# Two input queues, pairwise sums of squares, earlier forget gates, a chunked mixer start and a PSUM sum in the tail, in one layer of a hybrid encoder

## The chip, the cores and the metric

The kernel runs on one core of one Trainium2 chip. The metric is the device time of one execution in microseconds, as the median of several runs. A core has five engines that each work through their own list of instructions in order: TensorE (PE, matmuls), VectorE (DVE), ScalarE (ACT), GpSimd (POOL) and SyncE (SP, here only for issuing DMAs). They wait for one another by semaphores.

## The reference

One layer for 512 prompt tokens and 64 sample tokens (T = 576), model width 1024. The sample tokens also attend to 1024 cached rows.

```
h = rmsnorm(x, g_attn)
q, k, v, f_lin, q_c, c_kv, k_r = split(h @ w_in)
logf = log_sigmoid(f_lin + b_f)                 # forget gates, 8 heads
F = cumsum(past logf, then logf)
fox = softmax(mask(q k^T / 8 + F[t] - F[s])) v  # 8 heads of 64
mla = latent attention with rotary key, from q_c, c_kv, k_r
x = x + concat(fox, mla) @ w_out
u = rmsnorm(x, g_ffn) @ w_up                    # gate | value, 2 x 2816
x = x + (silu(conv3(gate)) * conv3(value)) @ w_down
y = rmsnorm(x, final_norm)
outputs: y, and the new k, v, logf, latent, rope key, conv rows
```

## The kernel before

Everything is kept transposed: features lie on the 128 partitions, the 576 tokens along the free axis. The width 1024 is eight chunks of 128. Every fp32 product is made of three PE passes over split values: each operand is written as a high half (rounded, type fp32r) and a low half (the remainder), and `gemm` (L201) adds low x high, high x high and high x low in one PSUM bank. `hilo` (L192) splits a weight tile: ACT writes the high half (L194), DVE or POOL the low half (L135, chosen by the tables `ENG` and by counting). `split_scaled` does the same for activations, with the norm's gain multiplied in (L266 on ACT, L267 on DVE). Weight tiles arrive in two buffers `wr` and are split into two buffers `wh`.

The start: SP issues the loads of the eight input tiles `x_in`, of `par` (gains), of `w_krf` (rope key and forget weights) and of the first key weights `wk`, in turn, then constants `con`, cached keys and values, and further weights. As the chunks arrive they are split into `xs` tiles, and two gemms run chunk by chunk: the one with 72 columns for the rope key and the forget logits, and `k0`, the keys of the first pair of heads. ACT squares the eight chunks (L220), DVE and POOL add them up in two groups of four (L135), and `col_sums` (L230) adds over the partitions with a matmul against ones. `rstd` makes from this the factor R = 1/rms with Ln, Exp and one Newton step (L250 to L262); all evacuations of the projections multiply by R. While that runs, PE works on the next projections, which need no R.

`fox_gemm(p)` (L447) makes keys, queries and values of pair p of the eight FoX heads; `gates` (L559) turns the forget logits into log-sigmoid, its running sum by a scan, and the tile `cf`, whose high and low halves are added to the scores by matmuls (L523) with the selector `sl`. The scan of the cached forget values (L585) reads `sp`, loaded over the same buffer as `con`. `s_gemm` (L743), `s_scores`, `s_values` and others are generators that issue their work in small steps; a planner with costs mixes them, so that projection matmuls fill the gaps between score and value steps. The framework's scheduler then fixes the order on each engine. In this phase the projections write two PSUM banks named `g` in turn: a new gemm waits until DVE has evacuated the bank.

The mixer: after `w_out`, the eight chunks of x are split again (`x2hl`), the same norm is made (R2), and `up_conv` runs 44 tiles of `w_up`, gate and value alternately (tile ch and ch + 22). `down_group` collects the down projection. In the tail the last part of the down projection runs in two halves of the tokens (320 and 256), and for each of the eight output tiles m: DVE adds the PSUM result into x (L971), ACT squares it (L976), DVE adds to a running sum (L978), two matmuls against ones close the sum (L980, L981), then Ln, Exp and Newton make `r3`, and DVE (L996) or POOL (L993, L994) multiply and the result goes out by DMA (L997). In the second half POOL takes the tiles in `TPOOL`, here 0 and 1.

Of the kernel before, what the change touches and what calls it, by code (L numbers as in the profile page):

```python
# [7 lines left out]
F32 = mybir.dt.float32  # L8
# [7 lines left out]
P = 128  # L16
# [39 lines left out]
    "sq0": "a", "acc0": "gggvvv", "sq": "agv", "acc": "gvvv",  # L56
# [9 lines left out]
TPOOL = (0, 1)  # L66

W0 = 6
# [3 lines left out]
def build(nc, tc, io):  # L72
# [74 lines left out]
    S.preload_act_table_set("natural_log_exp_and_others")  # L147
    par = sb([P, N_PAR], F32, "par", 1)
    wkrf = sb([P, 1024], F32, "wr", 2)
    x_in = []  # L150
    for kc in range(8):
        xt = mixt()
        nc.sync.dma_start(xt[:, :T], io["xT"][:, kc, :])
        x_in.append(xt)
        if kc == 0:
            nc.sync.dma_start(par[:, :C_GF], io["par"][:, :C_GF])
            nc.sync.dma_start(wkrf[:, :144], io["w_krf"][:, :144])
            wk = sb([P, 1024], F32, "wr", 2)
        if kc == 1:
            nc.sync.dma_start(wkrf[:, 144:576], io["w_krf"][:, 144:])  # L160
            nc.sync.dma_start(wk[:, :512], io["w_in"][0][:, :512])
        if kc == 2:
            nc.sync.dma_start(wk[:, 512:], io["w_in"][0][:, 512:])
    nc.scalar.dma_start(par[:, C_GF:], io["par"][:, C_GF:])
# [36 lines left out]
    def gemm(ps, M, hl, acts, halves, by_chunk=False):  # L201
# [5 lines left out]
        for hf, kc in steps:  # L207
            o, w = halves[hf]
            for pi, (wi, xi) in enumerate(((0, 1), (0, 0), (1, 0))):
# [40 lines left out]
    def rstd_of(v, y, a, out):  # L250
        S.activation(y, v, AF.Ln)
        S.activation(y, y, AF.Exp, scale=-0.5)
        newton(v, y, a, out)

    def newton(v, y, a, out):
        V.tensor_tensor(a, y, y, op=ALU.mult)
        V.scalar_tensor_tensor(a, a, -0.5, v, op0=ALU.mult, op1=ALU.mult)
        V.scalar_tensor_tensor(out, a, 1.5, y, op0=ALU.add, op1=ALU.mult)

    def rstd(ps, n, out):  # L260
        v, y, a = (raw()[:, :T] for _ in range(3))
        evac(lambda d, p, c: V.tensor_scalar(d, p, 1.0 / n, EPS, op0=ALU.mult, op1=ALU.add), v, ps)  # L262
        rstd_of(v, y, a, out)
# [13 lines left out]
    for kc in range(8):  # L277
# [169 lines left out]
    def fox_gemm(p):  # L447
# [3 lines left out]
        G.dma_start(io["o_k"][p], k[:, :T])  # L451
        ps = in_tile(4 + p)
# [30 lines left out]
    def fox_setup(p, q, k, v):  # L483
# [14 lines left out]
        for hh in range(2):  # L498
            V.tensor_copy(sl[:, 64 * hh:64 * hh + 64], sel[:, 2 * p + hh:2 * p + hh + 1].to_broadcast([72, 64]))
# [598 lines left out]
```

## Time and profile before

| | |
|---|---|
| median of 3 runs | 811.48 us (809.47 to 812.81) |
| profiled execution | 810.69 us, span 808.9 us, mean granted clock 0.988 |
| PE busy | 772.8 us, 96% |
| DVE, ACT, POOL busy | 508.5, 340.6, 264.0 us |
| HBM read, written | 64.1 MB, 5.5 MB |

The page gives busy time per engine, the list of waits names for each engine whom it waited for, the timeline gives single instructions with the idle time ahead of them in brackets, and the table of stretches gives busy time and granted clock between two times. A clock of 1.00 is 2.4 GHz, 0.50 is 1.2 GHz. Times in the rows count from the start of the span.

### The profile page before, as it was taken

Reading aid. Unit: us, or ns where it says so; the run is one execution under the profiler, and the core shown is the slowest. Engines: PE = TensorE matmul, PEld = TensorE weight load, DVE = VectorE, ACT = ScalarE, POOL = GpSimd, SP = SyncE. Lnnn points to the kernel's source line nnn. Section 1 sums busy time; section 2 is a strip of 40 time slices with the busy share of each in tenths; the row PEclk is TensorE's granted clock in tenths of the full one; section 3 lists DMA queues with packets and bytes.
Section 4 is the critical chain, followed back from the end, with each engine's and each line's share of the span. In section 5 each row is a group of like instructions: output and inputs, shape, how many; then the busy total and the mean of one; then the engine's idle time right before and its main releaser. Section 6 shows DMA issues by size and latency. Waiting matters only on the chain.

```text
span 808.9 us, 14256 instructions
## 1 busy us (share of the span) xinstructions
PE 772.8 (96%) x5582; PEld 743.3 (92%) x5582; DVE 508.5 (63%) x941; ACT 340.6 (42%) x611; POOL 264.0 (33%) x390
## 2 busy tenths in 40 slices
PE   8898999999899989999999999999999999999994
PEld 8796899897789879999999999999999999999993
DVE  6838554878677763457867524676425667675356
ACT  7224652457667864124443212343113433433231
POOL 5134342336143230223333221433222343332034
PEclk9998999999999999999999999999999999999997
DMA  9373423545563741222222223222232222222313
GB/s 329 111 212 109 109 84 106 145 107 169 129 152 80 185 131 30 80 79 79 72 85 68 79 92 105 79 79 60 79 98 80 103 80 79 79 66 83 105 40 117
DMA packets 33811, 83.98 MB, mean 104 GB/s; under 512 B 6006, under 2 KB 9350, under 8 KB 33744
## 3 DMA queue, kind: packets, MB, share of 16 engines
q1 hardware_dynamic: 31520, 78.55, 32.6%
q0 software_dynamic: 1008, 3.19, 1.1%
q10 hardware_dynamic: 1216, 1.33, 0.5%
q8 instruction: 44, 0.72, 0.4%
q14 instruction: 23, 0.19, 0.1%
HBM read 64.12 MB, written 5.49 MB: 86 GB/s over the span
## 4 chain that ended last, share of the span: by engine, by line
PE 76%; DVE 10%; ACT 5%; DMA 3%; issue 3%; SPq 1%; POOL 1%; DVEq 0%; ACTq 0%; POOLq 0%
PE g L210 31%; PE s L210 19%; PE t L210 12%; PE g L438 3%; PE g L969 1%; DMA mix<-xT 1%; DVE B L382 1%; DVE xs L267 1%; PE s L720 1%; PE t L375 1%; ACT p L326 1%; PE s L969 1%; DMA A<-qr 1%; PE s L522 1%; DVE raw L135 1%
## 5 line engine op out<-in xcount | busy, mean ns | idle before, releaser
L210 PE MATMUL g<-xs,wh 128*128 128x288 f32 (+2 forms) x2028 | 281.1, 295 | 0.3 <-ACT spt L128 0.2
L210 PEld LDWEIGHTS g<-xs,wh 128*128 128x128 f32 x2028 | 271.1, 189 | 1.7 <-ACT spt L128 0.4
L194 ACT ACTIVATE wh<-wr 128x1024 fp32r<-128x1024 f32 (+4 forms) x106 | 99.8, 942 | 204.3 <-PE g L210 88.4
L135 POOL TENSOR_TENSOR wh<-wr,wh 128x1024 fp32r<-128x1024 f32 (+3 forms) x51 | 111.8, 2192 | 216.5 <-ACT wh L194 173.7
L210 PE MATMUL s<-xs,wh 128*128 128x320 f32 (+3 forms) x840 | 121.1, 300 | 2.3 <-DVE xs L267 2.3
L210 PEld LDWEIGHTS s<-xs,wh 128*128 128x128 f32 (+1 forms) x840 | 116.3, 188 | 2.7 <-ACT wh L194 1.8
L210 PE MATMUL t<-xs,wh 128*128 128x256 f32 (+3 forms) x576 | 83.9, 296 | 1.2 <-DVE xs L267 1.2
L210 PEld LDWEIGHTS t<-xs,wh 128*128 128x128 f32 (+1 forms) x576 | 79.1, 188 | 1.6 <-DVE xs L267 1.4
L135 DVE TENSOR_TENSOR wh<-wr,wh 128x1024 fp32r<-128x1024 f32 (+5 forms) x55 | 59.0, 1077 | 13.7 <-ACT wh L194 13.4
L892 POOL COPY KR<-raw 128x2 f32<-128x2 f32 x33 | 14.6, 443 | 94.1 <-DVE raw L890 94.1
L332 POOL TENSOR_SCALAR p<-p,small 128x128 f32<-128x128 f32 (+2 forms) x48 | 27.5, 575 | 50.9 <-DVE small L327 40.8
L896 DVE SCALAR_TENSOR_TENSOR raw<-raw,par 128x578 f32<-128x578 f32 x22 | 33.6, 1526 | 14.0 <-ACT raw L895 14.0
L326 ACT ACTIVATE p<-s,small 128x128 f32<-128x128 f32 (+1 forms) x64 | 33.6, 527 | 12.5 <-DVE small L361 9.2
L920 ACT ACTIVATE raw<-raw 128x578 f32<-128x578 f32 x22 | 15.1, 688 | 54.5 <-DVE raw L897 54.5
L382 DVE TENSOR_TENSOR B<-t,B 128x512 fp32r<-128x512 f32 (+1 forms) x64 | 29.9, 482 | 9.3 <-ACT B L128 9.2
L128 ACT ACTIVATE B<-t 128x512 fp32r<-128x512 f32 (+1 forms) x64 | 26.2, 435 | 17.1 <-PE t L375 16.4
L361 DVE TENSOR_REDUCE small<-s 128x1 f32<-128x128 f32 (+1 forms) x64 | 30.5, 480 | 4.3 <-PE s L359 2.9
L896 DVE SCALAR_TENSOR_TENSOR raw<-pq,par,raw 128x578 f32<-128x578 f32 x11 | 22.7, 2059 | 12.4 <-ACT raw L895 12.4
L375 PE MATMUL t<-ident,p 128*128 128x128 f32 x160 | 29.1, 277 | 1.0 <-DVE B L382 0.5
L890 DVE TENSOR_TENSOR raw<-s,R 128x256 f32<-128x256 f32 x22 | 9.3, 424 | 31.8 <-PE s L210 31.8
L438 PE MATMUL g<-spt,sv 128*128 128x128 f32 x216 | 26.7, 276 | 0.3 <-ACT spt L128 0.2
L438 PEld LDWEIGHTS g<-spt,sv 128*128 128x128 f32 x216 | 25.2, 192 | 1.1 <-ACT spt L128 0.6
(337 smaller groups left out, 1344.1 us busy)
## 6 DMA issues: line engine op xcount, KB each, us to landing
wr<-w_up SPq DMA_DIRECT2D x44, 512.0 KB
wr<-w_dn SPq DMA_DIRECT2D x24, 384.0 KB
wr<-w_in SPq DMA_DIRECT2D x16, 512.0 KB
A<-pq SPq DMA_DIRECT2D x32, 256.0 KB
mix<-xT SPq DMA_DIRECT2D x16, 288.0 KB
wr<-w_out SPq DMA_DIRECT2D x8, 512.0 KB
A<-pq SPq DMA_DIRECT2D x24, 128.0 KB
sk<-k_c SPq DMA_DIRECT2D x4, 512.0 KB
```

What stands on the lines that cost most here:

```text
L128: S.activation(dst, src, AF.Copy)
L135: (V if pick(kind) == "v" else G).tensor_tensor(dst, a, b, op=op)
L194: S.activation(hl[:, 0, a:b], r[:, a:b], AF.Copy)
L210: PE.matmul(ps[hf][:M, :w], lhsT=hl[:, wi, kc * M:(kc + 1) * M], rhs=acts[kc][:, xi, o:o + w], start=(kc == 0 and pi == 0), stop=(kc == n ...
L326: S.activation(p, src, AF.Exp, bias=nm, accum_out=sm[:, 0:1])
L332: (G if e == "g" else V).tensor_scalar(p, p, sm[:, 1:2], 1.0, op0=ALU.mult, op1=ALU.mult)
L361: V.reduce_max(nm[:, 0:1], s[:, :W], axis=AX.X, negate=True)
L375: PE.transpose(t[:, P * (i - j):P * (i - j + 1)], st["p"][i][:, P * j:P * (j + 1)], ident)
L382: V.tensor_tensor(ptj[:, 1, off:], t[:, :w], f(ptj[:, 0, off:]), op=ALU.subtract)
L438: PE.matmul(out, lhsT=v[:, j, :], rhs=spt[:, j, :], start=(j == 0), stop=(j == 8))
L896: V.scalar_tensor_tensor(t, u[:, 1:579], par[:, C_CW + 44 + ch:C_CW + 44 + ch + 1], t, op0=ALU.mult, op1=ALU.add)
L969: PE.matmul(ps[:, :w], lhsT=whl[m][:, wi, kc * P:(kc + 1) * P], rhs=g2[kc][:, xi, c], start=(kc == 0 and pi == 0), stop=(kc == n - 1 and p ...
```

## The change

1. The input comes by two queues: SP issues the eight input tiles, ACT issues `par`, `w_krf` and `wk`, ahead of its table load. The further weights on SP stand behind constants and caches.
2. The high halves of `wk` are written by POOL (`hilo` with `eng=G`). When chunks are taken one by one, the passes begin with high x high.
3. Squares are added by twos, all on DVE, and `col_sums` takes four tiles. `ident`, `bfc`, `sel` and the casts `sl` are made after R (`normed`).
4. `gates` runs between the keys and the queries of the second pair, in `mix` buffers.
5. `up_gemm` runs the mixer's tiles 0 and 22 chunk by chunk, with the norm's sums issued after the fourth chunk; the split x lies in buffers `sk`, `sv` and four of `xs`.
6. In the tail's second half the running sum lies in a PSUM bank, `r3` is written to PSUM and copied by ACT for POOL, and POOL takes three tiles.

```diff
-    "sq0": "a", "acc0": "gggvvv", "sq": "agv", "acc": "gvvv",
+    "sq0": "a", "acc0": "v", "sq": "agv", "acc": "gvvv",
-TPOOL = (0, 1)
+TPOOL = (0, 1, 2)
-W0 = 6
+W0 = 5
...
+    wk = sb([P, 1024], F32, "wr", 2)
+    nc.scalar.dma_start(par[:, :C_GF], io["par"][:, :C_GF])
+    nc.scalar.dma_start(wkrf[:, :144], io["w_krf"][:, :144])
+    nc.scalar.dma_start(wk[:, :512], io["w_in"][0][:, :512])
+    nc.scalar.dma_start(wkrf[:, 144:576], io["w_krf"][:, 144:])
+    nc.scalar.dma_start(wk[:, 512:], io["w_in"][0][:, 512:])
+    S.preload_act_table_set("natural_log_exp_and_others")
...
+        if eng is G:
+            G.tensor_scalar(hl[:, 0, a:b], r[:, a:b], 1.0, 1.0, op0=ALU.mult, op1=ALU.mult)
+        else:
+            S.activation(hl[:, 0, a:b], r[:, a:b], AF.Copy)
...
-            for pi, (wi, xi) in enumerate(((0, 1), (0, 0), (1, 0))):
+            for pi, (wi, xi) in enumerate(((0, 0), (0, 1), (1, 0)) if by_chunk else ((0, 1), (0, 0), (1, 0))):
...
-            hilo(hk, wk, 0, 512)
+            hilo(hk, wk, 0, 512, G)
-            hilo(hk, wk, 512, 1024)
+            hilo(hk, wk, 512, 1024, G)
...
-        rstd(col_sums([sq_sum([t[:, :T] for t in x_in[n:n + 4]], "sq0", "acc0") for n in (0, 4)]), D, R)
+        normed = rstd(col_sums([sq_sum([t[:, :T] for t in x_in[n:n + 2]], "sq0", "acc0") for n in (0, 2, 4, 6)]), D, R)
+    with tc.issue_after(normed):
+        V.tensor_copy(ident, con[:, K_ID:K_ID + P])
+        V.tensor_copy(bfc, con[:, 0:320])
+        V.tensor_copy(sel, con[0:72, K_SEL:K_SEL + 8])
...
         G.dma_start(io["o_k"][p], k[:, :T])
+        if between:
+            between()
         ps = in_tile(4 + p)
...
-            fx[p] = fox_gemm(p)
-            if p == 1:
-                gates()
+            fx[p] = fox_gemm(p, gates if p == 1 else None)
...
+    XT = [("sk", 2), ("sk", 2), ("sv", 2), ("sv", 2)] + [("xs", 8)] * 4
...
+    def up_gemm(chs):
+        hls = [wload(io["w_up"][ch], 1024) for ch in chs]
+        pss = [psg() for _ in chs]
+        for kc in range(8):
+            if kc == 4:
+                rstd(sumsq(x2), D, R2)
+            for hl, ps in zip(hls, pss):
+                for hf, (o, w) in enumerate(HB):
+                    for pi, (wi, xi) in enumerate(((0, 1), (0, 0), (1, 0))):
+                        PE.matmul(ps[hf][:, :w], lhsT=hl[:, wi, kc * P:(kc + 1) * P], rhs=x2hl[kc][:, xi, o:o + w],
+                                  start=(kc == 0 and pi == 0), stop=(kc == 7 and pi == 2))
+        return dict(zip(chs, pss))
...
+    early.update(up_gemm((0, NCH)))
...
+        run = bank("s")[:, :w] if hf else acc
...
-                    V.tensor_tensor(acc, acc, sq, op=ALU.add)
+                    V.tensor_tensor(acc if m == 6 else run, run, sq, op=ALU.add)
...
+        if hf:
+            newton(v, y, a, pn[:, :w])
+            S.activation(r3, pn[:, :w], AF.Copy)
+            r3, r3g = pn[:, :w], r3
```

How the built program stands, at three places. On POOL at the start, where the tiles are memory that is set to zero for later use, and `ISA` is an instruction that selects POOL's code library; before:

```order
L380 MEMSET B 128x2x128
L492 MEMSET sv 64x128
L135 ISA
L135 TENSOR_TENSOR raw<-raw 128x576
L583 DMA sp<-logf_c 8x1024
L135 TENSOR_TENSOR raw<-raw 128x576 x2
```

and after the change:

```order
L382 MEMSET B 128x2x128
L190 ISA
L190 TENSOR_SCALAR wh<-wr 128x512
L496 MEMSET sv 64x128
L190 TENSOR_SCALAR wh<-wr 128x512
L135 TENSOR_TENSOR wh<-wr,wh 128x1024
L588 DMA sp<-logf_c 8x1024
```

The library instruction now stands ahead of the high halves of `wk`, and the DMA of the cached forget values behind a weight split.

On DVE a few evacuations behind R, the last of which frees the bank `g` for the second pair's keys (`raw<-g,R` are evacuations of the projections, `pq` the split keys and queries); before:

```order
L450 TENSOR_TENSOR raw<-g,R 128x288
L454 SCALAR_TENSOR_TENSOR raw<-t,R 128x288
L454 SCALAR_TENSOR_TENSOR raw<-s,R 128x288
L135 TENSOR_TENSOR wh<-wr,wh 128x1024
L489 COPY sk<-raw 128x64
L467 TENSOR_TENSOR pq<-raw,pq 128x512
L457 TENSOR_TENSOR raw<-g,R 128x288
```

and after the change:

```order
L452 TENSOR_TENSOR raw<-g,R 128x288
L458 SCALAR_TENSOR_TENSOR raw<-t,R 128x288
L504 CAST sl<-sel 72x64 x4
L458 SCALAR_TENSOR_TENSOR raw<-s,R 128x288
L590 SCALAR_TENSOR_TENSOR spt<-sp,B 8x1024
L493 COPY sk<-raw 128x64
L567 SCALAR_TENSOR_TENSOR mix<-mix 8x576
L471 TENSOR_TENSOR pq<-raw,pq 128x512
L461 TENSOR_TENSOR raw<-g,R 128x288
```

The casts `sl`, the scan of the cached forget values (L590) and the first gate step (L567) now stand ahead of the evacuation that frees the bank `g`; the three copies of constants, not shown, stand directly behind R. Before, the copies, the casts and the scan stood ahead of R.

On PE between the cached-key scores of the first head (`s<-sk,qb`) and the matmul that adds the forget terms (`s<-cf,sl`); before:

```order
L522 MATMUL s<-sk,qb 128x320
L210 MATMUL g<-xs,wh 128x288 x144
L341 MATMUL t<-ident,raw 128x128 x4
L494 MATMUL t<-ident,raw 64x128
L210 MATMUL g<-xs,wh 128x288 x27
L341 MATMUL t<-ident,raw 128x128 x4
L210 MATMUL g<-xs,wh 128x288 x10
L494 MATMUL t<-ident,raw 64x128
L210 MATMUL g<-xs,wh 128x288 x11
L523 MATMUL s<-cf,sl 128x384 x2
```

and after the change:

```order
L527 MATMUL s<-sk,qb 128x320
L208 MATMUL g<-xs,wh 128x288 x72
L343 MATMUL t<-ident,raw 128x128 x4
L498 MATMUL t<-ident,raw 64x128
L528 MATMUL s<-cf,sl 128x384 x2
L528 MATMUL s<-cf,sl 128x320
L530 LDWEIGHTS bfc
L530 MATMUL s<-bfc 128x64
L208 MATMUL g<-xs,wh 128x288 x72
L520 MATMUL s<-A 128x256
```

The forget terms now follow 72 projection matmuls instead of 192, and 72 more stand behind them, ahead of the first head's own scores.

## Rows read from the trace of the kernel before

**Rows 1.** The page, busy us by engine: share of the span, instructions.

```profile
PE 772.8 (96%) x5582; PEld 743.3 (92%) x5582; DVE 508.5 (63%) x941; ACT 340.6 (42%) x611; POOL 264.0 (33%) x390
```

**Rows 2.** Waits of PE: for whom, us in total, times, longest.

```profile
PE s L523 <- DVE cf L590: 3.1, 1, 3.1
PE s L230 <- DVE raw L135: 2.9, 1, 2.9
...
PE t L210 <- DVE xs L267: 1.2, 1, 1.2
```

**Rows 3.** Stretches: us, busy by engine, granted clock, DMA share, GB/s.

```profile
24.50:27.70 3.20, 3.20 (x7) 2.32 (x8) 1.48 (x2) 0.00 (x0) 0.00 (x0) 0.50 0.31 92
73.00:79.00 6.00, 5.97 (x23) 4.54 (x23) 4.45 (x17) 3.08 (x10) 2.92 (x6) 0.50 0.47 132
180.00:320.00 140.00, 129.17 (x866) 113.61 (x865) 99.18 (x255) 96.80 (x247) 44.77 (x68) 1.00 0.48 128
```

**Rows 4.** Timeline of PE at the start: start us, us, instruction [idle before].

```profile
6.62 0.46 PE L210 MATMUL s<-xs,wh 128*72 128x288 f32 x2 [1.68 <-DVE xs L267]
...
24.44 3.24 PE L230 MATMUL s<-raw,ones 128*128 128x288 f32 x6 [2.89 <-DVE raw L135]
...
34.04 6.26 PE L210 MATMUL g<-xs,wh 128*128 128x288 f32 x46
```

**Rows 5.** Timeline of POOL at the start.

```profile
7.10 0.20 POOL L492 MEMSET sv<- 64x128 f32 x1
15.34 1.42 POOL L135 TENSOR_TENSOR raw<-raw 128x576 f32<-128x576 f32 x1 [8.03 <-ACT raw L220]
```

**Rows 6.** Timeline of DVE around R.

```profile
18.71 5.67 DVE L135 TENSOR_TENSOR raw<-raw 128x576 f32<-128x576 f32 x3
...
28.09 2.27 DVE L585 TENSOR_TENSOR_SCAN spt<-sp,B 8x1024 f32<-8x1024 f32 x1
...
32.63 0.45 DVE L320 TENSOR_TENSOR mix<-s,R 32x288 f32<-32x288 f32 x1
...
37.61 0.45 DVE L457 TENSOR_TENSOR raw<-g,R 128x288 f32<-128x288 f32 x1
...
40.34 0.46 DVE L457 TENSOR_TENSOR raw<-g,R 128x288 f32<-128x288 f32 x1 [1.67 <-PE g L210]
```

**Rows 7.** Line L499 alone: ns of one, least, median, most.

```profile
L499 DVE CAST sl<-sel x8: 179/186/1854, 15.4 to 96.3; 72x64 fp32r<-72x64 f32 x8
```

**Rows 8.** DMA in the first 30 us: a queue, and an issue with its landing.

```profile
q8 instruction: 1, 0.02, 0.2%
...
sp<-logf_c POOLq DMA_DIRECT2D x1, 32.0 KB, 5.9
```

**Rows 9.** Timelines of PE and DVE between R and the gates.

```profile
41.72 18.55 PE L210 MATMUL g<-xs,wh 128*128 128x288 f32 x137
...
59.34 0.74 DVE L562 SCALAR_TENSOR_TENSOR raw<-mix 8x576 f32<-8x576 f32 x1
```

**Rows 10.** Timelines of ACT and DVE, a weight split after the mixer's start.

```profile
384.38 1.06 ACT L194 ACTIVATE wh<-wr 128x1024 fp32r<-128x1024 f32 x1 [1.58 <-PE s L210]
...
385.47 1.23 DVE L135 TENSOR_TENSOR wh<-wr,wh 128x1024 fp32r<-128x1024 f32 x1 [0.29 <-ACT wh L194]
```

**Rows 11.** Timelines of DVE, PE, POOL and ACT in the tail.

```profile
796.05 1.02 DVE L978 TENSOR_TENSOR raw<-raw 128x256 f32<-128x256 f32 x1 [0.48 <-ACT raw L976]
796.99 0.41 DVE L971 TENSOR_TENSOR mix<-s,mix 128x256 f32<-128x256 f32 x1
797.12 0.70 PE L980 MATMUL o<-raw,ones 128*128 128x256 f32 x2 [1.54 <-DVE raw L978]
...
801.04 1.35 DVE L996 SCALAR_TENSOR_TENSOR v<-mix,par,v 128x256 f32<-128x256 f32 x2
801.17 1.79 POOL L994 TENSOR_TENSOR raw<-mix,v 128x256 f32<-128x256 f32 x2 [2.55 <-DVE v L258]
804.47 0.38 ACTq L997 DMA_DIRECT2D o_y<-raw  x1
```

More of the change, by code (lines that the diff above doesn't have):

```diff
@@ L154, in build @@
         x_in.append(xt)
[L155 to L164, printed above, removed]
+    nc.sync.dma_start(par[:, C_GF:], io["par"][:, C_GF:])
     con = sb([P, 1152], F32, "sp", 1)
@@ L252, in rstd_of @@
         S.activation(y, y, AF.Exp, scale=-0.5)
-        newton(v, y, a, out)
+        return newton(v, y, a, out)
     def newton(v, y, a, out):
@@ L257, in newton @@
         V.scalar_tensor_tensor(a, a, -0.5, v, op0=ALU.mult, op1=ALU.mult)
-        V.scalar_tensor_tensor(out, a, 1.5, y, op0=ALU.add, op1=ALU.mult)
+        return V.scalar_tensor_tensor(out, a, 1.5, y, op0=ALU.add, op1=ALU.mult).ins
     def rstd(ps, n, out):
@@ L262, in rstd @@
         evac(lambda d, p, c: V.tensor_scalar(d, p, 1.0 / n, EPS, op0=ALU.mult, op1=ALU.add), v, ps)
-        rstd_of(v, y, a, out)
+        return rstd_of(v, y, a, out)
     def split_scaled(dst, src, g):
@@ L445, in build, with fox_gemm @@
     mixes = [None] * 8
-    def fox_gemm(p):
+    def fox_gemm(p, between=None):
         ps = k0 if p == 0 else in_tile(p)
@@ L497, in fox_setup @@
         sl = sb([72, P], F32R, "sl", 2)
-        for hh in range(2):
-            V.tensor_copy(sl[:, 64 * hh:64 * hh + 64], sel[:, 2 * p + hh:2 * p + hh + 1].to_broadcast([72, 64]))
+        with tc.issue_after(normed):
+            for hh in range(2):
+                V.tensor_copy(sl[:, 64 * hh:64 * hh + 64], sel[:, 2 * p + hh:2 * p + hh + 1].to_broadcast([72, 64]))
         samples[p] = dict(sk=sk, sv=sv, qb=qb, sl=sl, mix=mix, cost=5, tags=SMP["F"])
@@ L560, in gates @@
         S.activation(z, z, AF.Identity, bias=bf)
-        mn = raw()[:8, :T]
+        mn = mixt()[:8]
         V.scalar_tensor_tensor(mn, z, -1.0, z, op0=ALU.mult, op1=ALU.min)
-        e = raw()[:8, :T]
+        e = mixt()[:8]
         S.activation(e, mn, AF.Exp)
-        up = raw()[:8, :T]
+        up = mixt()[:8]
         V.tensor_scalar(up, e, 1.0, None, op0=ALU.add)
@@ L877, in build @@
     R2 = sb([P, T], F32, "R", 1)
-    rstd(sumsq(x2), D, R2)
     cs = sb([P, 512], F32, "KR", 1)[:, :176].rearrange("p (a b) -> p a b", b=4)
-    def up_conv(ch):
-        hl = wload(io["w_up"][ch], 1024)
-        ps = psg()
-        gemm(ps, P, hl, x2hl, HB)
+    def up_gemm(chs):
[10 more added lines that the diff above has]
+        return dict(zip(chs, pss))
+    early = {}
+    def up_conv(ch):
+        ps = early.pop(ch, None)
+        if ps is None:
+            hl = wload(io["w_up"][ch], 1024)
+            ps = psg()
+            gemm(ps, P, hl, x2hl, HB)
         u = raw()
@@ L898, in up_conv @@
         return t
-    gslots = [("A", 2, 1), ("A", 2, 1), ("B", 2, 2), ("B", 2, 2)] + [(t, 2, 1) for t in ("sk", "sk", "sv", "sv")] + [(t, 1, 1) for t in ("cf", "sp", "spt")]
+    gslots = [("A", 2, 1), ("A", 2, 1), ("B", 2, 2), ("B", 2, 2)] + [("xs", 8, 1)] * 4 + [(t, 1, 1) for t in ("cf", "sp", "spt")]
     gq = []
@@ L950, in build @@
         nc.sync.dma_start(r[:, :n * P], io["w_dn3"][m])
-        t = xst()
+        t = sb([P, 2, T], F32R, *XT[m])
         S.activation(t[:, 0, :n * P], r[:, :n * P], AF.Copy)
@@ L972, in build @@
             if m == 0:
-                S.activation(acc, x2[m][:, c], AF.Square)
+                S.activation(run, x2[m][:, c], AF.Square)
             else:
@@ L985, in build @@
         S.activation(y, y, AF.Exp, scale=-0.5)
-        newton(v, y, a, r3)
+        if hf:
+            newton(v, y, a, pn[:, :w])
+            S.activation(r3, pn[:, :w], AF.Copy)
+            r3, r3g = pn[:, :w], r3
+        else:
+            newton(v, y, a, r3)
+            r3g = r3
         for k, mm in enumerate(TAIL[hf]):
```

15 lines of the change are left out of this document (5 added, 10 removed).

## The prediction

> **What bounds the kernel now.** I read the page first. TensorE (PE) is busy for 772.8 of 808.9 us [rows 1], so the whole kernel can win at most the 36.1 us in which PE stands still, plus what a lowered clock costs, minus any PE work added. No other engine comes near: VectorE (DVE) has 63%. So I read the list of what PE waited for [rows 2]: the longest waits are 3.1 us for DVE's `cf` (L590, the last step of the forget gates), 2.9 us for DVE's running sum of squares (L135), and 1.2 us for an `xs` tile when the mixer starts; the tail adds 1.5 us for DVE's L978 [rows 11]. The change works on these four places. Then I read the granted clock by stretch [rows 3]: behind the two longest waits PE ran busy at 0.50 (1.2 instead of 2.4 GHz), 24.5–27.7 and 73–79 us. Each of the two waits therefore cost more than its length. The largest store of idle time, 10.8 us of the stretch from 180 to 320 us (140.0 less 129.2 busy), lies in the MLA part, where the change puts a few neighbours in another order and nothing else.
>
> The sum is made against the profiled execution, 810.69 us (span 808.9 and 1.8 around it). The median of the runs is 811.48, so 0.8 comes on top at the end.
>
> **Start: input, keys, sum of squares.** Before, the first projection matmul runs at 6.62 after 1.68 us of idle [rows 4]. In the new order PE's first matmul is one of k0, and reads `wk`'s high half, which GpSimd (POOL) now makes. POOL reaches that point behind its memsets at about 7.1–7.3 [rows 5]. A 128x512 copy on POOL isn't in the trace; I take 0.4 to 0.7 us, between its 0.2–0.3 us memsets and 1.42 us for a two-input add on 576 columns [rows 5]. So PE begins at about 7.7, and waits about 1 us more for the low half of the first input tile, since DVE's queue has the `wk` low half ahead of it. From there PE has 96 matmuls at 0.136 us (46 took 6.26 [rows 4]), 13 us without further waits by my walk through the queues, so these gemms end at about 21.4. Before, they ended at about 21.5 with two of the next matmuls done (24.44 less the wait of 2.89 [rows 4]). That the input is issued from two queues I count at nothing: PE had work without a gap once it was under way, so tiles that land earlier are not waited for.
>
> Then the sum of squares. Before, three adds on DVE took 5.67 us [rows 6] next to POOL's adds, PE stood still for 2.9 us, and the last six records of the column sums took 3.24 at half clock [rows 4]. Now four independent adds of two tiles, each at most 1.9 (5.67/3), all on DVE, follow ACT's squares and end near 20 by my walk, before PE asks. The column sums double: eight fp32 matmuls, sixteen records at 0.27 (3.24/6 halved), about 4 us instead of 2 at full clock. They end at 25.4; before, at 27.7. As two of the 96 projection matmuls that follow had been done earlier before, 2.0 us are gained here.
>
> Less of that arrives. The constants, the casts `sl` and the scan of the cached forget logits (L585) stood ahead of R on DVE; now they stand behind it, ahead of the evacuation of `g` that frees the bank for the gemm of the second pair's keys. Before, DVE was idle 1.67 us ahead of that point and PE never noticed; that gemm began at 41.72 [rows 6, 9]. From the end of the column sums to the first use of R it took 32.63 − 27.68 = 4.95 [rows 4, 6], of which about 0.6 was the scan in the way; so R stands at 29.7. Behind it on DVE: the evacuations and splits that also stood there before, up to and with that evacuation (32.63 to 38.06, less a weight split of 1.2 that now stands earlier: 4.2 us [rows 6, 10]), the three copies of constants 0.5 (three small ones like the casts), four casts at 0.18 alone or 0.85 beside POOL's add (0.7 to 3.4 us; the row has 179 to 1854 ns [rows 7]), the scan 2.27 [rows 6], and the first gate step 0.74 [rows 9]: 8.4 to 11.1 us, to 38.1–40.8. A second bound gives the same: the logits' DMA is issued only after `sel` is copied (30.3), took 5.9 us to land [rows 8], and 4.3 us of DVE work follow it: 40.5. PE arrives at 25.4 + 12.8 + 1.6 (the cached-key scores) = 39.8. I take 40.4 for the gemm, a gain of 1.3; for the chance that the longer idle at the start (2.8 us, against 2.9 that lowered the clock later and 1.68 that didn't) costs half clock for some 3 us I take off 0.3. **Start: −1.0** (from −2.0 to +1.0).
>
> **Gates.** Before, the gates are queued on DVE after the whole of the second pair: first step at 59.34 [rows 9], some 12 us before PE can go on, and PE comes to L523 with 192 gemm matmuls done and waits 3.1 us [rows 2]. Now they are queued behind that pair's keys. By the same walk `cf` is there at 49.6–50.2, while PE has 72 matmuls (9.8 us) and five transposes between the cached-key scores and this point and reaches it at about 51; a gap of half a microsecond either way is possible. So 3.1 goes. The six microseconds at half clock after it [rows 3] had PE full (5.97); at full clock they would need 3.0, but the score chain of the first heads may then wait for ACT and DVE. I take half, 1.5, with 0 and 3.0 as bounds. 72 further matmuls now stand as filler behind that line (L528 in the changed kernel). **Gates: −4.6** (from −6.1 to −2.6).
>
> **Mixer start.** The 1.2 us wait [rows 2] goes, because tiles 0 and 22 now run chunk by chunk while the `xs` tiles come in. But both weight buffers are then held to the end of both tiles; the high half of the next weights takes ACT 1.06 and the low half DVE 1.23 [rows 10], and only 0.8 us of PE work are left when the first buffer comes free. PE waits about 1.0–1.2 there. **0** (−1.0 to +1.2). The `xs` tiles in other buffers cost nothing that I can find: their readers are long done.
>
> **Tail.** DVE's running sum takes 1.02 with both operands in SBUF beside POOL's multiplications; the evacuation behind it, with one operand in PSUM, takes 0.41 in the same stretch [rows 11], so I price the sum in PSUM at 0.4. Then the last tile is taken when its matmul ends, at 795.6 (797.12 less 1.54), instead of 796.99, and r3 comes 1.4 earlier. Behind r3: ACT's copy adds 0.4 before POOL and DVE can both go; POOL has three products instead of two at 0.9 (1.79/2), DVE five instead of six at 0.4 to 0.67 (1.35/2) [rows 11]; the last output DMA goes at about 3.2 after r3 instead of 3.5 (804.47). **Tail: −1.7** (−1.2 to −2.3).
>
> **The sum.** −1.0 − 4.6 + 0 − 1.7 = −7.3; 810.69 − 7.3 = 803.4, against the median **804.2**. The other order in the MLA part I set at 0, with 2 us either way.
>
> **Rivals.**
> *POOL's first call is dear (slower side).* Ahead of POOL's first arithmetic the built program has a library-reload instruction. Before it fell into an idle stretch of 8.03 us that ended with a wait for ACT [rows 5], so its cost can be anything from 0 to 8 us; now PE's first matmul waits behind it. For: it is the first arithmetic there. Against: in the first 30 us the instruction queue moved one packet of 0.02 MB [rows 8], no sign of code being fetched. If it takes x us, PE starts x later; the wait for the low half (1.0) vanishes in it, and the idle is long enough for 3 us at half clock (1.6 lost): the time is 804.2 + x + 0.6, slower than before from x = 6.7 on, 812.8 at 8.0.
> The Trainium skill (GPSIMD Engine Reference, section 2.1 Instruction dispatch) speaks for it: a first call to a freshly loaded POOL kernel pays an instruction-memory load of about 6 us that no profile instruction shows. An estimate by that figure would be 804.2 + 6.0 + 0.6 = 810.8. The 8.03 us of idle can neither confirm nor exclude it.
> *The gates' wait comes back.* DVE's queue between 30 and 50 us is now full; if the logits' DMA lands 3 us later than I take, the gemm at 40.4 and `cf` move by as much. That gives 807.2. For: everything there hangs on one DMA issued late. Against: the DMA share is low there, and 5.9 us was measured with full queues.
> *The MLA part eats the gain.* Its idle time hangs on chains of score, exponential and transpose; another phase of ACT and DVE can cost 3 to 5 us: 807–809. For: 10.8 us idle show how tight it is. Against: the order there is nearly the same.
>
> **How the numbers follow.** Forecast (801 to 807.4) 0.55; better than that, with the half-clock stretch wholly won and no new waits (down to 799), 0.07; POOL's first call 0.15 (half of it short, 806–810); the gates' wait back 0.13 (about half under 807.4); the MLA part 0.10. The range from 800.0 to 811.5 leaves out about 1 in 10 above and fewer below. A measurement here tells about 0.5%, 4.1 us: faster is under 807.4. 0.55 + 0.07 + 0.06 + 0.04 = 0.72 faster; slower than 815.5 needs the full first call and another loss, 0.05; the rest 0.23.
>
> **What would show it.** PE's first projection matmul at 7.7 (not 11–16); no idle ahead of the column sums and granted clock 1.00 at 22–26; the second pair's key gemm at 40.4; L528 without a wait over 1 us and clock 1.00 after it; about 1 us of PE idle at 382–384; the `v` copy of r3 near 800. A first matmul after 10 us, or a DVE wait for the logits' DMA beyond 37 us, would make the prediction wrong.

## The result and the profile after

The changed kernel takes 814.36 us (median of 20 runs, 810.85 to 818.86), the kernel before 808.01 us in the same sessions (20 runs, 806.30 to 812.81). The ratio is 1.0076, interval 1.0061 to 1.0092: slower by 6.1 us, where 804.2 and a gain of 7.3 had been forecast. The three runs known ahead of the prediction, median 811.48, are among the slower of the 20. The profiled execution of before (810.69) lies 2.7 us above their median; the one of after (span 812.5, run 814.31) at its median.

The page of after, answering to [rows 1], and what PE waited for, answering to [rows 2]:

```profile
PE 777.2 (96%) x5590; PEld 748.5 (92%) x5590; DVE 501.1 (62%) x941; ACT 339.8 (42%) x610; POOL 259.2 (32%) x391
```

```profile
PE t L377 <- DVE B L384: 5.4, 4, 3.8
PE g L673 <- ACT raw L650: 3.6, 1, 3.6
PE o L208 <- POOL wh L190: 3.1, 1, 3.1
PE o L392 <- DVE mix L396: 2.1, 1, 2.1
```

The four waits that the change aimed at are gone or short. And yet PE stands still for 812.5 − 777.2 = 35.3 us, before 36.1: other waits took their place, and PE's own work took 4.4 us longer, 2.0 of it the doubled column sums. Most of the rest goes with the clock. The stretches of after at half clock, with the granted clock as the third number from the right (us, busy by engine, clock, DMA share, GB/s):

```profile
8.60:12.00 3.40, 3.16 (x12) 2.72 (x13) 3.37 (x5) 2.70 (x5) 1.28 (x2) 0.52 1.06 390
98.00:104.00 6.00, 5.46 (x23) 5.42 (x24) 2.19 (x7) 2.35 (x5) 2.24 (x4) 0.50 0.12 49
220.00:223.50 3.50, 3.50 (x11) 2.85 (x10) 2.77 (x7) 1.82 (x6) 0.00 (x0) 0.55 0.46 153
234.30:237.50 3.20, 3.20 (x11) 2.73 (x12) 2.83 (x9) 1.07 (x2) 0.00 (x0) 0.51 0.32 90
282.00:285.00 3.00, 2.89 (x12) 2.80 (x12) 1.82 (x7) 2.04 (x9) 0.48 (x1) 0.50 1.03 220
```

Five stretches, where before had the two of [rows 3]. The first is the start of the program, and each of the others stands behind one or two waits of PE. Where the time went is seen best from a few points that both kernels pass (starts in us, from the timelines):

| point | before | after | gates alone | gates, mixer, tail |
|---|---|---|---|---|
| gemm of the second pair's keys | 41.72 | 41.84 | 39.85 | 37.98 |
| first MLA score matmul (L701, in after L706) | 212.5 | 210.6 | | |
| first evacuation of `w_out` | 323.8 | 330.4 | 314.8 | 313.4 |
| evacuation of the last tile in the tail | 797.0 | 800.3 | 788.0 | 783.3 |
| end of the span | 808.9 | 812.5 | 799.9 | 794.7 |

After is 0.1 behind at the first point, 1.9 ahead when the MLA scores begin, and 6.6 behind when `w_out` begins: 8.5 us are lost in the MLA part, where the change was supposed to do nothing. Mixer start and tail then win 3 us back. The first row needs care: one execution of one start isn't the next. Six traces of kernels with the old start (before, e3, e8, e11, e12, e14 below) reach that gemm at 37.98 to 41.72, median 39.6, and before is the slowest of them; four with the new start (after, e1, e4, e13) at 41.84 to 42.15. The PE waits in question, first in the FoX part, then in the MLA part:

```profile
98.54 0.69 PE L377 MATMUL t<-ident,p 128*128 128x128 f32 x2 [3.82 <-DVE B L384]
...
218.99 1.78 PE L673 MATMUL g<-xs,wh 128*128 128x512 f32 x6 [3.60 <-ACT raw L650]
...
234.20 0.77 PE L392 MATMUL o<-B,v 128*128 128x512 f32 x1 [2.14 <-DVE mix L396]
```

What ACT did ahead of the second one, in after (L641 and L643 cast the cached rope keys into `cf`, L650 evacuates a query gemm):

```profile
216.26 1.11 ACT L641 ACTIVATE cf<-spt 32x1088 fp32r<-32x1088 f32 x1 [3.37 <-DMA spt<-kr_T]
217.39 1.11 ACT L643 ACTIVATE cf<-spt 32x1088 fp32r<-32x1088 f32 x1
218.53 0.41 ACT L650 ACTIVATE raw<-g 128x288 f32<-128x288 f32 x1
```

and in before (the same lines are L636, L638 and L645):

```profile
215.18 0.41 ACT L645 ACTIVATE raw<-g 128x288 f32<-128x288 f32 x1 [0.33 <-PE g L210]
218.01 1.11 ACT L636 ACTIVATE cf<-spt 32x1088 fp32r<-32x1088 f32 x1 [2.41 <-DMA spt<-kr_T]
219.14 1.11 ACT L638 ACTIVATE cf<-spt 32x1088 fp32r<-32x1088 f32 x1
```

In before the evacuation goes first and frees a bank `g`, and PE has six matmuls to do while ACT waits for the DMA (and then waits 1.8 us for `cf`). In after the two casts stand ahead of it, ACT stands still 3.4 us for the DMA with the evacuation queued behind, and so does PE. The third wait, on DVE in after:

```profile
231.42 1.92 DVE L135 TENSOR_TENSOR wh<-wr,wh 128x512 fp32r<-128x512 f32 x1
233.37 0.68 DVE L396 TENSOR_TENSOR mix<-o,mix 64x512 f32<-64x512 f32 x1
```

A weight's low half (L135) stands ahead of what PE waits for. Before, POOL wrote it (229.32 to 230.63), and DVE was free of it. The first wait, on DVE's `B` at 98.54, has a like cause. DVE in after, then POOL:

```profile
93.64 2.88 DVE L307 TENSOR_TENSOR raw<-mix,raw 32x576 f32<-32x576 f32 x1 [1.05 <-DMA raw<-cos]
```

```profile
93.55 2.36 POOL L135 TENSOR_TENSOR wh<-wr,wh 128x1024 fp32r<-128x1024 f32 x1
```

A step of the rotary key (L307) waits for a DMA and then takes 2.88 us beside a weight's low half on POOL; in e1, where no such half stands beside it, it takes 0.74. `B` (L384) stands behind it on DVE. The same number stands behind all three (e1 below has none of them): `W0`, the weight from which the low halves alternate between POOL and DVE, went from 6 to 5, and with it every later weight changed its engine.

### The profile page after: what moved, and what is told of

The parts are those of the page before. It is cut to its first block, busy times and chain, and to the rows that moved or that the text cites. A ratio compares the mean times of both kernels' runs of the same rounds, so it can differ in the third digit from the quotient of the medians.

```text
span 812.5 us, 14257 instructions
## 1 busy us (share of the span) xinstructions
PE 777.2 (96%) x5590; PEld 748.5 (92%) x5590; DVE 501.1 (62%) x941; ACT 339.8 (42%) x610; POOL 259.2 (32%) x391
## 4 chain that ended last, share of the span: by engine, by line
PE 84%; DVE 4%; DMA 4%; ACT 3%; SPq 2%; issue 1%; POOL 1%; POOLq 0%; ACTq 0%; DVEq 0%
PE g L208 36%; PE s L208 19%; PE t L208 13%; PE g L440 2%; PE s L725 1%; PE t L377 1%; PE g L994 1%; DMA A<-pq 1%; PE o L392 1%; PE s L994 1%; DVE B L384 1%; PE s L894 1%; PE t L994 1%; DVE xs L135 1%; PE g L673 1%
## 5 line engine op out<-in xcount | busy, mean ns | idle before, releaser
L208 PE MATMUL g<-xs,wh 128*128 128x288 f32 (+2 forms) x1680 | 240.1, 297 | 0.3 <-ACT wh L192 0.2
L208 PEld LDWEIGHTS g<-xs,wh 128*128 128x128 f32 x1680 | 229.0, 190 | 1.8 <-DVE raw L461 0.4
L135 POOL TENSOR_TENSOR wh<-wr,wh 128x1024 fp32r<-128x1024 f32 (+3 forms) x51 | 110.8, 2173 | 229.3 <-ACT wh L192 180.2
L192 ACT ACTIVATE wh<-wr 128x1024 fp32r<-128x1024 f32 (+4 forms) x104 | 98.5, 949 | 194.4 <-PE g L208 67.3
L135 DVE TENSOR_TENSOR wh<-wr,wh 128x1024 fp32r<-128x1024 f32 (+5 forms) x55 | 62.1, 1132 | 28.1 <-ACT wh L192 20.4
L208 PE MATMUL s<-xs,wh 128*128 128x320 f32 (+3 forms) x504 | 77.7, 299 | 0.2 <-DVE xs L265 0.2
L208 PEld LDWEIGHTS s<-xs,wh 128*128 128x128 f32 (+1 forms) x504 | 71.0, 186 | 0.9 <-DVE xs L265 0.6
L208 PE MATMUL t<-xs,wh 128*128 128x320 f32 (+3 forms) x348 | 53.5, 296 | 0.0
L208 PEld LDWEIGHTS t<-xs,wh 128*128 128x128 f32 (+1 forms) x348 | 48.3, 185 | 0.1
L384 DVE TENSOR_TENSOR B<-t,B 128x512 fp32r<-128x512 f32 (+1 forms) x64 | 30.0, 482 | 6.2 <-ACT B L128 5.9
L208 PE MATMUL s<-sk,wh 128*128 128x320 f32 (+1 forms) x192 | 31.8, 300 | 0.1
L208 PE MATMUL s<-sv,wh 128*128 128x320 f32 (+1 forms) x192 | 31.6, 300 | 0.0
L208 PE MATMUL g<-sk,wh 128*128 128x256 f32 (+1 forms) x186 | 29.6, 291 | 0.4 <-ACT wh L192 0.4
```

Source lines behind the costliest of these rows:

```text
L135: (V if pick(kind) == "v" else G).tensor_tensor(dst, a, b, op=op)
L208: PE.matmul(ps[hf][:M, :w], lhsT=hl[:, wi, kc * M:(kc + 1) * M], rhs=acts[kc][:, xi, o:o + w], start=(kc == 0 and pi == 0), stop=(kc == n ...
L384: V.tensor_tensor(ptj[:, 1, off:], t[:, :w], f(ptj[:, 0, off:]), op=ALU.subtract)
```

## The experiments

Each kernel ran beside the kernel before on the same chip. The ratio is to that kernel, with its 95% interval.

| run | kernel | us | ratio |
|---|---|---|---|
| e1 | changed, `W0` = 6 | 806.51 | 0.998 (0.996 to 0.9999) |
| e2 | before, `W0` = 5 | 820.46 | 1.0143 (1.0117 to 1.0169) |
| e3 | before + gates | 801.04 | 0.9907 (0.9887 to 0.9927) |
| e4 | before + start, `W0` = 6 | 814.49 | 1.0072 (1.0051 to 1.0093) |
| e5 | before, `W0` = 5 for FoX only | 813.17 | 1.0051 (1.0033 to 1.0068) |
| e6 | before + pairs, constants behind R | 813.81 | 1.0054 (1.0036 to 1.0072) |
| e7 | before + queues | 809.96 | 1.0013 (0.9995 to 1.003) |
| e8 | before + gates, mixer, tail | 796.55 | 0.9843 (0.9817 to 0.987) |
| e9 | e8 + pairs, constants behind R | 800.16 | 0.9897 (0.9871 to 0.9923) |
| e10 | e8 + queues | 799.70 | 0.988 (0.9853 to 0.9907) |
| e11 | before + tail | 808.11 | 0.9989 (0.9971 to 1.0007) |
| e12 | before + mixer | 806.11 | 0.9974 (0.9958 to 0.9989) |
| e13 | changed, `cf` casts on POOL | 808.92 | 0.9999 (0.9986 to 1.0012) |
| e14 | e8, `cf` casts on POOL | 798.38 | 0.9861 (0.9837 to 0.9884) |
| e15 | e8 + pairs, constants ahead of R | 801.70 | 0.99 (0.9881 to 0.9918) |

**One number.** e1 and e2:

```diff
-W0 = 5
+W0 = 6
```

> The changed kernel with W0 set back from 5 to 6 and nothing else; that number decides at which weight tile the alternation of DVE and POOL for the low halves begins, so that every later weight's low half goes back to the engine it had in the kernel before. Theory A (the swapped engines give another order in the MLA part, and that order loses the 8.5 us by which the changed kernel falls back between 210 and 304 us): 814.4 - 8.5, about 806 us (804 to 808), no PE wait over 2 us after 200 us. Theory B (the order is incidental, the MLA part loses because everything before it is shifted by the start and the gates): still 812 to 815 us.

> The kernel before with W0 = 5 and nothing else. Theory A: the MLA part gets the swapped engines without any other part of the change: 808.0 plus 5 to 9, 813 to 817 us, with half-clock stretches between 210 and 300 us. Theory B: one alternation more or less is nothing: 807 to 809 us.

Theory A. Setting `W0` back takes 7.9 us off the changed kernel and puts it 1.6 us below the kernel before; setting it to 5 in the kernel before costs 11.7, more than I expected. With `W0` = 6 the changed kernel's instructions stand in the old order on every engine in the MLA part, and its one long wait there is the 2.0 us for `cf` that before has too (1.8). In the kernel before with `W0` = 5 the two MLA waits of after come up again, at the same lines, behind a longer wait for the gates:

```profile
PE s L523 <- DVE cf L590: 3.7, 1, 3.7
PE g L668 <- ACT raw L645: 3.3, 1, 3.3
PE o L390 <- DVE mix L394: 2.1, 1, 2.1
```

**Which weights.** e5 is e2 with one turn of the alternation skipped at the first MLA weight:

```diff
+        if not ml.get("flip"):
+            ml["flip"] = pick("wA")
         hl = wload(io["w_qu"][u], 384)
```

> The kernel before with W0 = 5, but with one turn of the alternation skipped ahead of the first MLA weight, so that the FoX weights have swapped engines and the MLA weights those of the kernel before (its order on all engines is that of before from the first MLA weight on). Theory A1 (what costs 11.7 us in the run with W0 = 5 are the MLA weights): 808 to 812 us. Theory A2 (the swapped FoX weights cost it): 816 to 820 us. Half-clock time after 200 us: none by A1, about 6.8 us by A2.

813.17: 7.3 of the 11.7 us come from the MLA weights, 4.4 stay with the FoX weights, just above the span that A1 had given. In e5's trace the wait for the gates is 3.7 us instead of 3.1.

**What PE waits for in the MLA part.** e13 moves the two casts to POOL and leaves ACT's queue free:

```diff
-        S.activation(KS[0:32, :KEYS], krc[:, :KEYS], AF.Copy)
+        G.tensor_scalar(KS[0:32, :KEYS], krc[:, :KEYS], 1.0, 1.0, op0=ALU.mult, op1=ALU.mult)
```

> The changed kernel with the two casts of the cached rope keys into cf moved from ACT to POOL, and nothing else (its order differs from the changed kernel's only around these casts). In the changed kernel ACT stands at the first of them for a DMA from 213 to 216 us, with the evacuation of a query gemm queued behind, and PE waits 3.6 us for that evacuation (219.0) and then runs at half clock. Theory F (ACT's queue order behind that DMA is what PE waits for): the 3.6 us wait falls to under 1.5 us and the half-clock stretch at 219 goes: 809 to 811 us. Theory G (the chain from the DMA to cf itself is late, the evacuation only stands in the same place): PE waits as long for cf, now from POOL: 813 to 816 us.

> Earlier gates, chunked mixer and PSUM tail (796.6 us) with the same two casts on POOL. There ACT has the evacuation ahead of the casts, and PE waits 1.9 us for cf with 3.4 us at half clock at about that place. Theory F: little to gain in the order, 795.5 to 797. Theory G: POOL is slower than ACT's 1.11 us per cast, PE waits 1 us more: 797 to 799.

In the changed kernel this gives 5.4 us, theory F; the clock reads 1.00 from 219 to 222.5, and of the wait of 3.6 us this is left:

```profile
PE s L726 <- POOL cf L643: 1.1, 1, 1.1
```

So ACT's queue order behind a late DMA was the mechanism of that wait, and most of what the MLA weights cost came with it. The third wait, on `mix`, is gone too, though the weight's low half still stands ahead of it on DVE: here it takes 0.68 us in place of 1.92. In the order of e8, where ACT has the evacuation ahead anyway, the same edit gains nothing: e14 is 1.8 us slower, in G's span but inside the two intervals, and G's mechanism isn't seen (PE waits 1.3 us for `cf`, in e8 1.9). An edit that repairs one order does nothing for the other.

**The gates alone.** e3 is the kernel before with this, and with `gates` in `mix` buffers as in the change:

```diff
-            fx[p] = fox_gemm(p)
-            if p == 1:
-                gates()
+            fx[p] = fox_gemm(p, gates if p == 1 else None)
```

> The kernel before with the earlier gates alone; its built order differs from before only between 45 and about 120 us. Theory A: the 3.1 us wait at 68.7 us and most of the half-clock stretch behind it go, a PE wait of some size may come back near 95 us when fewer filler matmuls are left: 803 to 806 us. Theory B: the whole gain is given back later: 807 to 809 us.

801.04, 7.8 us less, better than theory A's span. PE reaches L523 without a wait, and the stretch of [rows 3] at half clock is not there: 60 to 80 us read 20.00 us busy at 1.00. In this trace the column sums are a lesson of their own:

```profile
24.25 1.72 PE L230 MATMUL s<-raw,ones 128*128 128x288 f32 x6 [2.91 <-DVE raw L135]
```

The start is that of the kernel before, the wait the same 2.9 us, but the six records take 1.72 instead of the 3.24 of [rows 4]: this time the clock stayed up. By the gemm of the second pair's keys the profiled execution of before was 1.9 us slower than this one. The wait itself isn't firm either: with the same order e11, e12 and e14 wait 0.7 us here and e8 not at all.

**The start.** e4 is all of the new start, e6 and e7 its two halves (squares by twos with the constants behind R; two queues with POOL's halves of `wk`). The core of e6, then of e7:

```diff
-    "sq0": "a", "acc0": "gggvvv", "sq": "agv", "acc": "gvvv",
+    "sq0": "a", "acc0": "v", "sq": "agv", "acc": "gvvv",
-        rstd(col_sums([sq_sum([t[:, :T] for t in x_in[n:n + 4]], "sq0", "acc0") for n in (0, 4)]), D, R)
+        normed = rstd(col_sums([sq_sum([t[:, :T] for t in x_in[n:n + 2]], "sq0", "acc0") for n in (0, 2, 4, 6)]), D, R)
+    with tc.issue_after(normed):
+        V.tensor_copy(ident, con[:, K_ID:K_ID + P])
```

```diff
+    nc.scalar.dma_start(wk[:, :512], io["w_in"][0][:, :512])
-            hilo(hk, wk, 0, 512)
+            hilo(hk, wk, 0, 512, G)
```

> The kernel before with the new start alone (two queues, high halves of wk on POOL, pairwise squares, constants behind R) and W0 = 6, so that the later weights keep their engines. The second pair's key gemm began at 41.84 us in the changed kernel and at 41.72 before, so by both theories this is 807.0 to 809.0 us by that stretch; by theory B a shift of phase alone may cost up to 4 us more.

> The kernel before with the squares added by twos on DVE and the constants behind R, and nothing else (W0 = 6, input on one queue). The 2.9 us wait ahead of the column sums goes, 2.0 us of column sums are added. Theory C (the start's loss of 5.7 us lies in the two queues and POOL's part): 806 to 808.5 us. Theory D (it lies in the constants and the scan behind R, which crowd DVE up to the gates): 811 to 814 us.

> The kernel before with the input on two queues, the high halves of wk on POOL and the passes beginning with high x high, and nothing else. The gemms of the chunks ended 2.7 us later in the changed kernel (23.3 against 20.6). Theory C: 811 to 815 us, with the first projection matmul at 8.2 to 8.7 us. Theory D: 807 to 810 us.

The new start costs 5.7 us; I had expected nothing. Theory C falls: the queues cost 1.3 (not clear of zero), the pairs 5.2. In the changed kernel one sees what each half does at its own place. PE, then POOL:

```profile
8.65 0.55 PE L208 MATMUL o<-xs,wh 128*128 128x288 f32 x1 [3.07 <-POOL wh L190]
...
23.31 4.04 PE L228 MATMUL s<-raw,ones 128*128 128x288 f32 x16
...
41.84 3.43 PE L208 MATMUL g<-xs,wh 128*128 128x288 f32 x24
```

```profile
6.71 0.32 POOL L382 MEMSET B<- 128x256 f32 x1
7.98 0.61 POOL L190 TENSOR_SCALAR wh<-wr 128x512 fp32r<-128x512 f32 x1 [0.96 <-DMA wr<-w_in]
```

POOL waited for the first half of `wk`, issued at 1.67, until 7.98, while the eight input tiles were under way and the DMA engines were busy throughout (share 1.00 from 4 to 8 us). So PE, which in the new order begins with `k0`, starts at 8.65 instead of 6.62 (before, with the 72-column gemm), in this execution at half clock; in e1, e4 and e13, with the same start, at 8.0 to 8.2 and full clock. The pairs do remove the wait ahead of the column sums. What they cost lies further on. In part it is the clock: the median granted clock of e6's runs is 0.983, that of the kernel before beside them 0.988, and 0.005 of 812 us is some 4 us of full clock (an estimate). In which stretch is less plain than it looks. Behind the gates' wait, 3.15 us in e6 and 3.13 in before, e6 runs at

```profile
70.50:84.00 13.50, 13.50 (x48) 9.90 (x48) 7.95 (x27) 6.89 (x21) 7.17 (x11) 0.50 0.56 129
```

and before, over as long a stretch, at

```profile
72.00:85.00 13.00, 11.81 (x57) 8.60 (x57) 8.20 (x28) 8.15 (x24) 7.04 (x11) 0.74 0.61 142
```

The same wait brings some 7 us at half clock in one and some 13.5 in the other, a difference of over 3 us of work, and e4 reads 0.50 from 72 to 85 as well. But e11 (before with another tail, below), whose instructions up to the tail stand in the order of the kernel before on every engine, does the same behind a wait of 3.14 us:

```profile
70.00:83.00 13.00, 12.88 (x46) 9.45 (x47) 7.97 (x28) 7.00 (x20) 7.32 (x11) 0.50 0.57 132
```

So the long stretch is not a mark of the pairs; what decides its length the rows don't say. Against e11's trace, e6 is 0.3 us behind at the second pair's key gemm, 2.4 at the first MLA score matmul and 4.1 at the first evacuation of `w_out`: PE waits 1.6 us in place of 0.4 for ACT's exponentials (L517, in e11 L515) and runs at half clock once more behind the wait for `cf` (0.72 from 223 to 229).

If the gates' wait were all of it, the pairs would be harmless once that is gone. e9 is e6's edit on e8, e10 is e7's edit on e8, and e15 is e9 with the three copies from `con`, the casts and the scan left where they were, ahead of R:

> Earlier gates, chunked mixer and PSUM tail (796.6 us without it) plus the squares by twos with the constants behind R. Theory E (alone on the kernel before the pairs cost 5.2 us because the half-clock stretch behind the gates' wait lasted 13.7 instead of 6.8 us and the MLA part lost more; without that wait this falls away): 795 to 799 us. Theory D (the constants, casts and the scan behind R crowd DVE where the earlier gates need it, so that PE waits between 75 and 110 us): 801 to 806 us, with waits for ACT's exponentials and a half-clock stretch near 100 us as in the changed kernel with W0 = 6.

> Earlier gates, chunked mixer and PSUM tail plus the two input queues, the high halves of wk on POOL and high x high first. Alone on the kernel before these cost 1.3 us. Theory D: 797 to 799 us, so that of the 10 us between this base (796.6) and the changed kernel with W0 = 6 (806.5) nearly all lies with the pairs. Theory E: the queues' later first matmul (8.2 instead of 6.6) shifts all by 2 to 3 us: 799 to 802.

> Earlier gates, chunked mixer and PSUM tail with the squares by twos, but the constants, casts and the scan left ahead of R as in the kernel before. With these behind R it was 800.2, without the pairs 796.6. Theory D (what stands behind R crowds DVE): 796 to 797.5. Theory H (the pairs themselves cost: eight column-sum matmuls instead of four, 2.0 us of PE, and the 2.9 us wait they remove had been slack or comes back elsewhere): 799 to 801.

They are not harmless: on e8 the pairs cost 3.6 us, a little less than theory D's span and more than E's, the queues 3.1 (in E's span, but the intervals of e8 and e10 overlap). And what stands behind R isn't the cause: with the constants ahead of R the pairs cost 5.1, theory H. Two of these are the four further column-sum matmuls. The clock has no part in it here (median 0.996 in e9, 0.992 in e15, 0.991 in e8). The profiles show besides that with `W0` = 6 every kernel that has both the pairs and the early gates makes PE wait for ACT's exponentials (L326 in before), mostly between 70 and 105 us: 3.0 us in e1, 1.9 in e9, 2.5 in e15, here e15:

```profile
PE s L517 <- ACT p L326: 2.5, 3, 1.4
```

In e8, without the pairs, the wait at this line is 0.4. The 2.0 us of column sums and the 1.5 us more of this wait would make up e9's 3.6 (an estimate from the rows; no run changes one without the other). Both halves together cost 10.0 us on e8 (e1 less e8), 3.3 more than the two apart, which is within what the intervals allow. How the pairs bring ACT behind there, and whether the halves do more together, stays open.

**Mixer and tail.** e8 is e3 with both, e11 has the tail alone (part 6 of the change), e12 the mixer start alone (part 5). Their cores, the tail's first:

```diff
-TPOOL = (0, 1)
+TPOOL = (0, 1, 2)
+        run = bank("s")[:, :w] if hf else acc
```

```diff
+    early.update(up_gemm((0, NCH)))
```

> The kernel before with the earlier gates, the chunked mixer start and the tail's sum in PSUM; the start and W0 are those of before. The gates alone gave 801.0. The mixer start saved 0.8 us of idle in the changed kernel (1.18 less 0.40), the tail about 1.1 (13.3 to 12.3 us from the last tile's matmul to the end): 799 us (797.5 to 800.5). If mixer and tail bring nothing of their own: 801.

> The kernel before with the tail's sum in PSUM, r3 in PSUM and three tiles on POOL alone. From the last tile's matmul to the end the changed kernel took 12.3 us instead of 13.3: 0.8 to 1.5 us less than before, 807.2 to 808.0. My term in the prediction was 1.7.

> The kernel before with the chunked mixer start alone. Gates, mixer and tail together gave 796.6, the gates alone 801.0; with about 1.2 for the tail, 2 to 3 us are left for the mixer: 805.5 to 807. My term in the prediction was 0 with a loss of 1 us as new idle: then 808 to 809.

The mixer start brings 3.0 us (0.9 to 3.4 by the ratio's interval), the tail 1.0, which its interval doesn't separate from nothing. On the gates both together bring 4.5, more than I expected. The traces give the two separately. From the first evacuation of `w_out` to the end of the tail's last projection matmul it is 471.7 us in before, e3 and e11, and 469.8 in after, e8 and e12: the mixer start is worth 1.9 us, 0.6 of it idle time of PE and 1.3 busy time. In the changed kernel the mixer start shows this behind the two early tiles:

```profile
389.79 0.51 PE L208 MATMUL g<-sk,wh 128*128 128x256 f32 x2 [0.40 <-ACT wh L192]
```

The wait for the held weight buffers is 0.4 us. In the tail of after, DVE, then the last output DMA:

```profile
800.27 0.42 DVE L996 TENSOR_TENSOR mix<-s,mix 128x256 f32<-128x256 f32 x1
...
803.87 0.43 DVE L256 SCALAR_TENSOR_TENSOR o<-raw 128x256 f32<-128x256 f32 x1
```

```profile
806.96 0.40 SPq L1028 DMA_DIRECT2D o_y<-raw  x1
```

The last tile is taken as its matmul ends, r3 stands 4.0 us later, and the last DMA goes 6.7 us after the matmul instead of 8.9 [rows 11]. In after the outputs then needed 5.5 us from that issue to the end of the span, before 4.4, and so 1.1 of 2.2 was left. From the end of the last tile's matmul to the end of the span it is 13.3 us in before, 12.2 in after, 11.7 in e11 and 11.5 in e8: the tail gives 1.1 to 1.9 us.

e8 beats both kernels: 796.55 us, 12.1 less than before in its session and some 18 less than the change as it was made.

## Why the prediction was wrong

**The MLA part, set at 0.** This is the step that failed most. The prediction said that the order there was nearly the same, and gave it 2 us either way; the third rival priced a shift of phase at 3 to 5. The diff had `W0 = 5` in two lines, and I costed them at nothing. 8.5 us went there in the trace, 7.9 in the timing (e1). It was not a shift of phase, as the rival had it: with the same start and the same gates, and the old engines, 1.8 of the 8.5 are left in e1's trace. What I took for nearly the same order had the two casts ahead of the evacuation on ACT; the built order would have shown it, and the trace of before showed that they wait for a DMA (its row at 218.01).

**The start, set at −1.0.** Measured alone +5.7 (e4), on e8 +10.0. Three things were mis-sized. The first matmul came at 8.65, not 7.7: I counted POOL's 0.6 us and not the DMA of `wk` that it waits for, and the gemms of the chunks ended at 23.3, not 21.4. (Before, they ended at 20.3: the 21.5 that I worked out from the wait holds, beside the two further matmuls, the first column-sum matmul as well.) The gain at the column sums was taken against a profiled execution whose sums ran at half clock, which those of e3, e8, e11, e12 and e14, with the same order, don't: against the median of the six, 39.6, the second pair's key gemm at 41.8 to 42.2 is a loss of some 2.4 us, where I forecast a gain of 1.3. And I looked only as far as that gemm; the waits for ACT's exponentials and the clock further on lay beyond it, and their cause is open. The DVE walk from R on held: R stood at 31.6 instead of 29.7, and the evacuation that frees the bank came 10 us later, inside my 8.4 to 11.1; but the scan ahead of it on DVE took 4.4 us, not 2.3 (35.62 to 40.06), and that was `W0` again: in e1 and e4, with no weight's low half on POOL beside it, it took 2.27.

**The gates, set at −4.6.** The mechanism was right and the size too small: −7.8 alone. L528 came without a wait (PE is busy for the whole of 40 to 80 us in the changed kernel at clock 1.00). I took half of the half-clock stretch as won; in e3 all of it was. That the stretch lasts 7 us in one execution of the old order and 13.5 in another puts the gates at 3.1 + 3.4 to 3.1 + 6.8 us (an estimate), and 7.8 lies between. In the changed kernel a good part went again at 94.7 to 98.5 us, where PE waits 3.8 us for DVE's `B` and then runs at half clock. That isn't the price of the filler spent earlier: e3 and e8, with the same gates, have no wait over 0.3 us between 70 and 105 us, and of the kernels with the early gates only after and e13, with `W0` = 5, have this one.

**The mixer start, set at 0.** −3.0 alone. The new idle was 0.4 us and not 1.0 to 1.2, because the wait for the next weights' high half was shorter than I had assumed. The traces show 1.9 of the 3.0: 0.6 less idle time and 1.3 less busy time, for which I had no term; the rest lies within e12's interval. Why PE is busy for less the rows don't show.

**The tail, set at −1.7.** The steps came as forecast up to the last issue (2.2 us earlier relative to the last matmul), of which 1.1 was kept in after, 1.6 in e11 and 1.9 in e8; timed alone −1.0 with zero inside its interval.

**The dear first call of POOL** was not the cause. Between POOL's last memset, which ends at 7.03, and its first arithmetic at 7.98 there is 0.95 us, put down to the DMA of `wk`. The Trainium skill's figure (GPSIMD Engine Reference, section 2.1 Instruction dispatch: about 6 us for a first call) is not seen here; the trace bounds it at under 1 us for this library and this instruction.

The rival that did come, a loss in the MLA part, had 0.10, and came by another cause than it named. Most of the time was lost in waits that weren't in the profile of before, because the change made them, and in the half clock behind them; the doubled column sums, 2.0 us, had been counted. Measured alone, start, gates, mixer, tail and `W0` add up to +1.8 us and not to the +6.1 of the whole: the start costs more beside the early gates than on the kernel before, and why stays open.

## What to carry to other kernels

A counter that alternates work between two engines is part of the order of everything that follows: moving its start by one swapped every later weight and cost 8 to 12 us, in parts that the change never meant to touch. Ahead of timing, compare the built order of the parts that should stay as they were, and look first at engines that have a DMA wait in their queue and at what is queued behind it. And take a change apart: here three of its six parts (gates, mixer, tail) gain 12 us together, and the start, with one number, loses 18. One trace is one execution: before a difference between two traces is put down to an edit, look at a third whose order is the same in that place.

## What the runs showed of the hardware

The same wait of PE didn't cost the same. Behind 2.9 us ahead of the column sums one execution ran at 0.50 and another, with the same code there, at full clock (3.24 against 1.72 us for six records); behind 3.1 to 3.3 us at the gates PE ran at half clock for some 7 us in before, e7 and e12 and for some 13.5 in e4, e6 and e11, of which before and e11 have the same order up to there. In e11 PE was busy for all 12 us from 71 to 83 and still at 0.50. So a wait of about 3 us cost from its own length to 7 us more, and what decided it is not shown.

An instruction with two inputs on DVE got longer beside one with two inputs on POOL. In the changed kernel, DVE, then POOL:

```profile
35.62 4.44 DVE L590 TENSOR_TENSOR_SCAN spt<-sp,B 8x1024 f32<-8x1024 f32 x1
```

```profile
35.49 2.42 POOL L135 TENSOR_TENSOR wh<-wr,wh 128x1024 fp32r<-128x1024 f32 x1
```

The scan takes 2.27 us in before and in e1, where POOL has nothing like it at that time. Here it ends at 40.06, 2.15 us after POOL's instruction (37.91), as if it had begun when that was done. The weight's low half at 231.42 takes 1.92 us and ends 0.55 after POOL's addition (230.96 to 232.79); in e13, with no such neighbour, it takes 0.68. The rotary step at 93.64 ends 0.61 after POOL's low half beside it; in e1, beside an instruction with one input on POOL, it takes 0.74. In each of the three the delay is nearly as long as the overlap.
